# New durations, a shared port and whole groups of small products in the count that orders a decoder trunk's engines

## The chip, the core and the metric

The kernel runs on one core of a Trainium2 chip. A core has five engines that run side by side, each through its own list of instructions in a fixed order: TensorE (PE, with its weight loads as PEld), VectorE (DVE), ScalarE (ACT), GpSimd (POOL) and SyncE (SP), which issues the transfers. The metric is the device time of one execution in microseconds (us), and of several runs the median.

## What is computed

A trunk of two layers (DEPTH = 2) over 1024 tokens of width 1024. Each layer normalises, projects the tokens with one large matrix, runs three token mixers, gates and merges their outputs, and projects back. The reference, cut to what matters here:

```python
def hybrid_layer(x, c_act, positions, ...):
    mod = c_act @ w_ada + b_ada
    shift, scale, gate = jnp.split(mod[:, None, :], 3, axis=-1)
    h = rms_norm(x, norm_g) * (1.0 + scale) + shift
    proj = h @ w_in
    pool_u, pool_g, q, k, v, ret_g, rw, rw_g, gate_logits = jnp.split(proj, points, axis=-1)
    o_pool = causal_pool_mixer(pool_u, pool_w, pool_scale) * jax.nn.silu(pool_g)
    o_ret = retention(q, k, v, positions, ret_norm_g) * jax.nn.silu(ret_g)
    o_rwkv = rwkv7_time_mix(rw, shift_mu, w0, w2, a0, a2, ...) * jax.nn.silu(rw_g)
    y = jnp.einsum('btnw,nwd->btnd', jnp.stack([o_pool, o_ret, o_rwkv], axis=2), w_branch)
    merged = jnp.sum(jax.nn.sigmoid(gate_logits.reshape(B, T, N_BRANCHES, D)) * y, axis=2)
    return x + gate * (merged @ w_out)

# inside rwkv7_time_mix, after r, w, k, v, a are made
    w = -jax.nn.softplus(-(w0 + jnp.tanh(wl) @ w2)) - 0.5
    a = jax.nn.sigmoid(a0 + al @ a2)
    def step(S, inp):
        r_t, w_t, k_t, v_t, a_t, b_t = inp
        sa = jnp.einsum('bhvk,bhk->bhv', S, a_t)
        S = S * w_t[:, :, None, :] + sa[..., None] * b_t[:, :, None, :] + v_t[..., None] * k_t[:, :, None, :]
        return S, jnp.einsum('bhvk,bhk->bhv', S, r_t)
```

The output is `rms_norm(x, final_g)` after both layers.

## The kernel before

**Large products.** The projections run as fp32r products of 128 columns of weights by 512 tokens into a PSUM tile `acc` (three banks). For accuracy each is made of three: high part by high part (`wh`, `hhi`), high by low (`hlo`), low by high (`wl`). The weights come by transfer into `wr`, ScalarE casts the high part `wh`, and GpSimd subtracts to get the low part `wl`. All three have three buffers. These products are the filler: they can run whenever an `acc` bank is free and weights are ready.

**Small products.** The RetNet heads (`ret_task`) and the RWKV head pairs (`rwkv_task`) use fp32 products and transposes of 128 by 128 or less, in PSUM tiles `mx` (two banks), `two` (two banks, used in turn by `cyt()`) and `ch`. An fp32 product appears as two rows of the profile, a transpose or an fp32r product as one. A RWKV head pair goes through these stages: `prepare` (low-rank products `lora_mm`, decay sums, normalising), `scores` (the products of BK and AR into an `mx` bank named `g` for the first head and a bank of `two` for the second), `invert` (a triangular inverse on VectorE), `states` (`av`), and then a chain of 16 chunks of 64 tokens. Each chunk is a serial walk: `two` from S and AR on TensorE, `xst` on VectorE, `ch` from xst and G on TensorE, `Z` on VectorE, `ch` from Z and BKt on TensorE, the new `S` on VectorE. There are eight such head pairs, four in each of the two layers.

**Which rows of the array.** In `lora_mm` the first output's products use partitions 0 to 63 of both operands and the second output's use 64 to 127, written in turn. The products in `scores` do the same with the two heads.

**The order.** After a first part whose order is written out by hand (line 230 in the profile), the kernel doesn't emit its instructions where they are written. A class `Log` records each call as an `Op` with its engine, operands and lane ("rwkv", "mix", "post", "evac" and so on, or "" for the main flow). At the end `plan()` simulates the five engines with one estimate of occupancy and latency for each operation, from `times()`, and always takes the earliest engine and on it the ready operation with the smallest key (its place in the log, with RWKV 3000 places ahead). VectorE, ScalarE and GpSimd may hold back an operation if a RWKV one is about to be ready. `emit()` then writes the instructions in the order of the simulated starts, at line 413, which is why most rows of the profile carry that line. The chip keeps this order on each engine, whatever the real times are: an operation that comes late holds up all that stand behind it on its engine.

The estimates of TensorE before: 227 ns for an fp32r product of 512 columns, scaled down to 256 columns, 120 below; `max(n * 0.846, m * 0.8) + 3` for any fp32 product or transpose; half of that if it uses 64 rows and writes 128; and 190 ns more until a reader may start. Weight transfers count 2200 ns.

Of the kernel before, what the change touches and what calls it, by code (L numbers as in the profile page):

```python
# [10 lines left out]
F32R = mybir.dt.float32r  # L11
# [6 lines left out]
P = 128  # L18
# [78 lines left out]
ORDER = ("PE", "DVE", "ACT", "POOL", "SP")  # L97
NEXT = {"PE": 54, "DVE": 34, "ACT": 34, "POOL": 78, "SP": 60}
BIAS = {"rwkv": -3000, "evac": -500, "post": -200, "ada": 1500}


class Op:
    __slots__ = (
        "eng", "fn", "args", "kw", "outs", "ins_", "lane", "key", "n", "late", "allocs", "after", "free",
        "left", "users", "ready", "start", "end", "occ", "dur", "inst", "no_dep", "own_dep", "idx",
# [78 lines left out]
class Log:  # L184


    def __init__(self, nc, tc):
        self.nc, self.tc = nc, tc
        self.on = False
        self.ops = []  # L190
        self.tag = {}
        self.acc = {}
        self.lane = ""
        self.vector = Proxy(self, "DVE", nc.vector)
        self.scalar = Proxy(self, "ACT", nc.scalar)
        self.gpsimd = Proxy(self, "POOL", nc.gpsimd)
        self.tensor = Proxy(self, "PE", nc.tensor)
        self.sync = Proxy(self, "SP", nc.sync)

    def call(self, eng, name, real, a, k):  # L200
# [4 lines left out]
        else:  # L205
            outs, ins = aps[:1], aps[1:]
        o = Op()
        o.eng, o.fn, o.args, o.kw, o.outs, o.ins_ = eng, real, a, k, outs, ins
        o.lane, o.n, o.late, o.inst = self.lane, name, not self.on, None
        o.no_dep = o.own_dep = None  # L210
        o.after, o.free, o.allocs = {}, [], []
        o.idx = len(self.ops)
        reads = ins + (outs if name == "matmul" and k.get("start") is False else [])
        for x, w in [(x, False) for x in reads] + [(x, True) for x in outs]:
# [12 lines left out]
            self.acc[x.tensor.name] = keep  # L227
        self.ops.append(o)
        if not self.on:
            o.inst = real(*a, **k)  # L230
        return o

    def times(self, o):
        out = o.outs[0]
        n = max(x.free_size() for x in o.outs + o.ins_)
        if o.eng == "PE":
            m = o.args[1].free_size() if o.n == "transpose" else o.kw["lhsT"].free_size()
            n = out.free_size()
            rows = (o.args[1] if o.n == "transpose" else o.kw["lhsT"]).partition_size()
            if o.n != "transpose" and o.kw["rhs"].dtype == F32R:  # L240
                occ = 227 * n / 512 if n >= 256 else 120
            else:
                occ = max(n * 0.846, m * 0.8) + 3
            if rows == 64 and out.partition_size() == P:
                occ /= 2
            return occ, occ + 190
        if o.eng == "SP":
            return 340, 2200
        if o.eng == "ACT":
            d = 215 + 0.75 * n + 45 * (len(o.ins_) - 1)  # L250
            return d - 95, d
        if o.eng == "POOL":
            if o.n == "memset":
                return 60 + n, 100 + n
            if n <= 16:
                d = (1650 if n > 4 else 1010) if len(o.ins_) > 1 else 190
            else:
                d = 190 + 2.15 * n
            return d - 45, d
        if o.n == "reciprocal":  # L260
            d = 240 + 5.86 * n
            return d - 80, d
        if o.n == "transpose":
            return 1960, 2030
        if o.n == "tensor_tensor_scan":
            return 185, 265
        wide = [x for x in o.ins_ if x.free_size() == n]
        d = 155 + 1.05 * n + 45 * (len(o.ins_) - len(wide))
        if len(wide) < 2 and all(x.space != PSUM for x in o.ins_ + o.outs):
            d = 170 + 0.62 * n  # L270
        return d - 84, d

    def plan(self):
# [39 lines left out]
        for o in todo:  # L313
            for p in o.after:
                p.users.append(o)
        cand = {e: [] for e in ORDER}
        free = {e: 0.0 for e in ORDER}
# [3 lines left out]
        def offer(o):  # L321

            for t in list(o.allocs):
# [87 lines left out]
    def emit(self):  # L411
        for o in self.plan():
            o.inst = o.fn(*o.args, **o.kw)  # L413
            if o.no_dep is not None:
# [11 lines left out]
def trunk_kernel(ctx, tc, xT, cvec, pos, vecs, consts, w_ada, w_all, pool_w, lora_w, out):  # L426
# [623 lines left out]
    def ret_task(l, hd, qT, kT, vT, sg):  # L1050
# [6 lines left out]
        for h in range(2):  # L1057
            cl = lambda t, c: t[:, c * P : (c + 1) * P]
            yield wait(kT[h], qT[h])
            ps = mx("rs")  # L1060
            for c in range(4):
                mmul(cl(ps, c), lhsT=cl(kT[h], c), rhs=cl(qT[h], c), start=True, stop=True)
            sm = mo("rsm")
# [3 lines left out]
            ps = mx("rkt")  # L1067
            for c in range(4):
                trans(cl(ps, c), cl(kT[h], c))
            kt = mo("rkt")  # L1070
# [3 lines left out]
            ps = mx("rvt")  # L1074
            for c in range(4):
                trans(cl(ps, c), cl(vT[h], c))
            vt = mo("rvt")
# [3 lines left out]
            kv = mx("rkv")  # L1081
            for c in range(4):
                mmul(cl(kv, c), lhsT=cl(kt, c), rhs=cl(vt, c), start=True, stop=True)
            R = []
# [21 lines left out]
            ps = mx("rot")  # L1106
            for c in range(4):
                trans(cl(ps, c), cl(yn, c))
            ob = mo("rob")
# [5 lines left out]
    def lora_mm(pss, lw, hc, lt):  # L1115
        for i, (a, b) in enumerate(((0, 0), (0, 1), (1, 0))):
            for j in range(2):
                own = slice(64 * j, 64 * j + 64)
                mmul(pss[j], lw[a][own, hc], lt[b][own, :], start=(i == 0), stop=(i == 2))

    def rwkv_task(l, hp, kT, rT, vp, lt, lw):
# [16 lines left out]
        def prepare(h):  # L1138
# [39 lines left out]
            ps = mx("vt")  # L1178
            for c in range(4):
                trans(ps[:, c * P : (c + 1) * P], vp[h][:, c * P : (c + 1) * P])  # L1180
            for par in range(2):
# [47 lines left out]
        def scores(h):  # L1229
            yield max(until(whole[h] + 1000), wait(Z, spare=600))  # L1230
            for q in range(2):
                ps = mx("bt")
                c0 = 8 * h + 4 * q
                for c in range(4):
                    trans(ps[:, c * P : (c + 1) * P], jt(BK, slice(0, P), c0 + c), timed=True)
# [61 lines left out]
        def states():  # L1297
            for q in range(4):
                yield wait(G, Z)
                ps = mx("av")  # L1300
                for j in range(8):
                    c, hd = 4 * q + j // 2, j % 2
                    mmul(
                        ps[0:64, j * 64 : j * 64 + 64],
                        G[64:128, 16 * hd + c, 64:128],
                        Z[64:128, c, 64 * hd : 64 * hd + 64],
                    )
                nc.scalar.copy(AV[:, q * HF : (q + 1) * HF], ps[0:64, :])
# [8 lines left out]
        for q in range(2):  # L1317
            ps = mx("m1")
            for u in range(16):
                uu = 16 * q + u  # L1320
                mmul(ps[32:64, u * 32 : u * 32 + 32], G[0:32, uu, 96:128], T13[:, uu, :], timed=True)
            nc.scalar.copy(T1[32:64, q * HF : (q + 1) * HF], ps[32:64, :])
# [4 lines left out]
        for q in range(2):  # L1327
            yield max(until(left[q]), 1500.0)
            ps = mx("m2")
            for u in range(16):  # L1330
                uu = 16 * q + u
                mmul(
                    ps[0:32, u * 32 : u * 32 + 32], T1[32:64, uu * 32 : uu * 32 + 32], G[32:64, uu, 96:128], timed=True
                )
            nc.scalar.copy(
# [58 lines left out]
    def rwkv_post(l, hp, h, yn, bv):  # L1394
        yield 6500
        yield wait(yn, spare=3000)
        ps = mx("yt")
        for j in range(4):
            trans(ps[:, j * P : (j + 1) * P], yn[:, j * P : (j + 1) * P])
        ob = t_ri("wob")  # L1400
# [828 lines left out]
```

## Times and profile before

| what | value |
|---|---|
| median of 3 runs | 2561.44 us (2560.07 to 2567.08) |
| profiled execution, its own time | 2556.54 us |
| its span, first to last instruction | 2554.8 us |
| mean granted TensorE clock | 0.967 |
| busy PE / DVE / POOL / ACT | 2420.8 / 1406.0 / 890.2 / 853.1 us |
| `acc` from hhi, wh: products, mean | 1788, 408 ns |

Rows of a group name the line, engine, operation, output and inputs, shape and count, then busy time, mean of one in ns, and the idle time just before them with its releaser. Matmuls are pipelined, so the duration of a row includes the way through the array; what a product costs TensorE is the distance from its start to the next start. Rows of a timeline give start, duration, engine and operation, and in brackets the idle time before and what ended it; "xN" merges N equal neighbours.

### The profile page before, as it was taken

The page shows a single profiled execution, that of the slowest core. Times are in us where ns is not written, and L with a number is a line of the kernel's source. Part 1 is how long each engine was busy: PE and PEld are TensorE (multiplying, and loading weights), DVE is VectorE, ACT ScalarE, POOL GpSimd, SP SyncE. Part 2 cuts the span into 40 slices and gives each one's busy share as a digit, 9 for nine tenths or more (in the row PEclk, how much of TensorE's full clock was granted, in tenths as well). Part 3 has the DMA queues.
Part 4 walks back from the last instruction along what each step waited for, and adds up shares of the span by engine and source line. Part 5 has one row for each costly group of instructions (what it writes and reads, how often), then busy time and mean ns, then how long its engine had stood idle before and what let it go on. Part 6 is the DMA issues. An engine that isn't in the chain of part 4 may idle for free.

```text
span 2554.8 us, 35214 instructions
## 1 busy us (share of the span) xinstructions
PE 2420.8 (95%) x13204; PEld 1963.2 (77%) x13204; DVE 1406.0 (55%) x2666; ACT 853.1 (33%) x1567; POOL 890.2 (35%) x772
## 2 busy tenths in 40 slices
PE   5998999998999999999989998999899999999998
PEld 4776777777777778788877876788778877887888
DVE  7675663674686370335365768525664765124354
ACT  5534322322322123512344342332242223342243
POOL 4211223223223343655442222133133244365641
PEclk9997999999999999999999998999899999999999
DMA  6312002112223362564562201121012124337542
GB/s 239 113 47 70 29 26 76 30 30 76 71 64 118 104 207 84 165 221 144 165 197 85 67 26 38 31 71 47 29 64 59 59 79 148 103 114 223 174 128 75
DMA packets 138043, 248.86 MB, mean 97 GB/s; under 512 B 15632, under 2 KB 18960, under 8 KB 137872
## 3 DMA queue, kind: packets, MB, share of 16 engines
q1 hardware_dynamic: 137872, 246.61, 30.7%
q8 instruction: 104, 1.70, 0.3%
q14 instruction: 67, 0.55, 0.1%
HBM read 187.04 MB, written 59.51 MB: 97 GB/s over the span
## 4 chain that ended last, share of the span: by engine, by line
PE 63%; DVE 9%; issue 1%; ACT 1%; DMA 1%; POOL 1%; DVEq 0%; SPq 0%; ACTq 0%; POOLq 0%
PE acc L413 52%; PE two L413 2%; PE ch L413 2%; PE m L413 1%; DVE two L413 1%; PE g L413 1%; DVE tm L413 1%; PE ro L413 1%; PE av L413 1%; DVE ksq L413 1%; DVE yc L413 0%; DVE traw L413 0%; DVE hlo L413 0%; DVE ada_acc L413 0%; DVE wsum L413 0%
## 5 line engine op out<-in xcount | busy, mean ns | idle before, releaser
L413 PE MATMUL acc<-hhi,wh 128*128 128x512 f32 x1788 | 728.8, 408 | 22.0 <-ACT gsg L413 11.6
L413 POOL TENSOR_TENSOR wl<-wr,wh 128x512 fp32r<-128x512 f32 x300 | 399.7, 1332 | 949.7 <-ACT wh L413 887.9
L413 PE MATMUL acc<-hlo,wh 128*128 128x512 f32 x1788 | 722.5, 404 | 0.0
L413 PE MATMUL acc<-hhi,wl 128*128 128x512 f32 x1788 | 721.6, 404 | 0.0
L413 PEld LDWEIGHTS acc<-hhi,wh 128*128 128x128 f32 x1788 | 342.4, 192 | 92.7 <-ACT gsg L413 12.7
L413 PEld LDWEIGHTS acc<-hhi,wl 128*128 128x128 f32 x1788 | 341.5, 191 | 66.3 <-issue 2.5
L413 PEld LDWEIGHTS acc<-hlo,wh 128*128 128x128 f32 x1788 | 342.0, 191 | 65.5 <-issue 4.0
L413 ACT CAST wh<-wr 128x512 fp32r<-128x512 f32 x300 | 185.4, 619 | 616.8 <-PE acc L413 463.6
L413 DVE SCALAR_TENSOR_TENSOR S<-ch,pc,SP 64x64 f32<-64x64 f32 x256 | 72.3, 282 | 60.0 <-PE ch L413 54.0
L413 ACT COPY y<-two 64x128 f32<-64x128 f32 x128 | 33.0, 258 | 215.3 <-PE two L413 210.1
L413 DVE TENSOR_TENSOR tm<-MT,two 64x30 f32<-64x30 f32 (+14 forms) x240 | 76.7, 319 | 21.1 <-ACT two L413 13.1
L413 DVE TENSOR_TENSOR two<-two,tm 64x30 f32<-64x30 f32 (+14 forms) x240 | 79.1, 330 | 8.3
L413 DVE SCALAR_TENSOR_TENSOR gs<-gs,acc 128x512 f32<-128x512 f32 x64 | 43.8, 684 | 71.0 <-PE acc L413 68.9
L413 PE MATMUL acc<-oz,wh 128*128 128x512 f32 x256 | 80.4, 395 | 0.0
L413 PE MATMUL acc<-oy,wh 128*128 128x512 f32 x256 | 80.3, 395 | 0.0
L413 PE MATMUL acc<-oG,wh 128*128 128x512 f32 x256 | 79.1, 390 | 0.0
L413 PEld LDWEIGHTS ch<-xst,G 128*65 128x65 f32 x512 | 46.9, 146 | 37.3 <-DVE xst L413 31.8
L413 ACT ACTIVATE gsg<-acc 128x512 f32<-128x512 f32 x86 | 50.7, 593 | 71.8 <-PE acc L413 48.0
L413 POOL TENSOR_TENSOR vr<-vr,fixed 128x8 f32<-128x8 f32 (+1 forms) x32 | 44.7, 1397 | 81.3 <-DVE vr L413 77.7
L413 PE MATMUL acc<-T,wh 128*128 128x512 f32 x216 | 67.6, 394 | 5.0 <-ACT acc L413 5.0
L413 DVE TENSOR_TENSOR xst<-two,MT 64x128 f32<-64x128 f32 x128 | 37.5, 293 | 61.8 <-PE two L413 56.3
L413 PEld LDWEIGHTS two<-S,AR 128*128 128x128 f32 x256 | 44.2, 202 | 35.1 <-DVE S L413 19.2
(334 smaller groups left out, 4507.5 us busy)
## 6 DMA issues: line engine op xcount, KB each, us to landing
wr<-in_w_all SPq DMA_DIRECT2D x328, 256.0 KB, 2.7
gd<-gsg SPq DMA_DIRECT2D x96, 256.0 KB, 2.0
gs<-gd SPq DMA_DIRECT2D x96, 256.0 KB, 3.8
wada<-in_w_ada SPq DMA_DIRECT2D x70, 256.0 KB, 2.9
ol<-od SPq DMA_DIRECT2D x48, 256.0 KB, 3.0
wraw<-in_w_all SPq DMA_DIRECT2D x36, 256.0 KB, 2.8
traw<-hd SPq DMA_DIRECT2D x32, 256.0 KB, 2.9
ringG<-in_w_ada SPq DMA_DIRECT2D x26, 256.0 KB, 4.8
```

The source lines that it names most:

```text
L413: o.inst = o.fn(*o.args, **o.kw)
```

## The change

The edit is in the class `Log` and in the places where small products are written.

1. **Durations.** `pe_time` replaces the TensorE estimates: 228 ns for more than 256 columns of fp32r, 120 otherwise; an fp32 product counts twice the old formula, a transpose once; half with 64 rows and 128 output partitions, as before. A reader may start 165 ns after, not 190.
2. **Port.** An operation has a flag `port`. It is set on GpSimd operations with more than one input, on VectorE operations with two full inputs in SBUF, and on VectorE copies and scalar operations with one input from SBUF. In the simulated run an operation with the flag waits until the last one with the flag has ended.
3. **Holding back.** ScalarE and GpSimd operations of the main flow (lane "") count as ready GUARD = 500 ns later. An operation that has been ready for PATIENCE = 2500 ns is no longer held back for RWKV. A GpSimd operation outside RWKV is put off if a VectorE operation of RWKV that needs the port will be ready within 0.7 of its duration.
4. **Units.** `with nc.together():` records all calls inside it as one `Op` with the sum of their times, ready when the inputs and banks of all are ready, and emitted without a gap. It is put around the products of `lora_mm`, the transposes and products of `ret_task`, the `vt`, `bt`, score, `av`, `m1` and `m2` products of `rwkv_task`, and the transposes of `rwkv_post`.

```diff
+GUARD = 500
+PATIENCE = 2500
...
+        o = self.group if self.on else None
+        if isinstance(o, Op):
+            o.calls.append((real, a, k, name))
+            o.outs += outs
+            o.ins_ += ins
+        else:
+            o = Op()
+            o.eng, o.calls, o.outs, o.ins_ = eng, [(real, a, k, name)], list(outs), list(ins)
...
+            if self.on and self.group is not None:
+                self.group = o
...
+    def pe_time(self, n, a, k):
+        out = a[0]
+        w = a[1] if n == "transpose" else k["lhsT"]
+        f = out.free_size()
+        if n != "transpose" and k["rhs"].dtype == F32R:
+            t = 228 if f > 256 else 120
+        else:
+            t = (max(f * 0.846, w.free_size() * 0.8) + 3) * (1 if n == "transpose" else 2)
+        return t / 2 if w.partition_size() == 64 and out.partition_size() == P else t
...
-            return occ, occ + 190
+            occ = sum(self.pe_time(q, a, k) for _, a, k, q in o.calls)
+            return occ, occ + 165
...
+            o.port = len(o.ins_) > 1
...
+        sb = [x for x in o.ins_ if x.free_size() == n and x.space != PSUM]
+        o.port = len(sb) > 1 or (len(sb) == 1 and len(o.ins_) == 1 and o.n in ("tensor_copy", "tensor_scalar", "tensor_scalar_mul"))
...
+            if o.lane == "" and o.eng in ("ACT", "POOL"):
+                o.ready += GUARD
             cand[o.eng].append(o)
...
-                    t = max(free[e], min(o.ready for o in cand[e]))
+                    t = max(free[e], min(max(o.ready, port) if o.port else o.ready for o in cand[e]))
...
-            now = [o for o in c if o.ready <= t]
+            now = [o for o in c if o.ready <= t and not (o.port and port > t)]
...
-            if e != "PE" and o.occ > 100:
+            if e != "PE" and o.occ > 100 and t < o.ready + PATIENCE:
                 soon = [h for h in c if h.lane == "rwkv" and h.key < o.key and t < h.ready < t + 0.7 * o.occ]
+                if e == "POOL" and o.lane != "rwkv":
+                    other = [h for h in cand["DVE"] if h.lane == "rwkv" and h.port and h.ready < t + 0.7 * o.occ]
+                    if other:
+                        o.ready = max(t, min(h.ready for h in other)) + 300
+                        continue
...
+            if o.port:
+                port = t + o.occ
...
     def lora_mm(pss, lw, hc, lt):
-        for i, (a, b) in enumerate(((0, 0), (0, 1), (1, 0))):
-            for j in range(2):
-                own = slice(64 * j, 64 * j + 64)
-                mmul(pss[j], lw[a][own, hc], lt[b][own, :], start=(i == 0), stop=(i == 2))
+        with nc.together():
+            for i, (a, b) in enumerate(((0, 0), (0, 1), (1, 0))):
+                for j in range(2):
+                    own = slice(64 * j, 64 * j + 64)
+                    mmul(pss[j], lw[a][own, hc], lt[b][own, :], start=(i == 0), stop=(i == 2))
...
-                for j in range(4):
-                    for hd in range(2):
-                        rows = slice(64 * hd, 64 * hd + 64)
-                        mmul(gps[hd][:, j * P : (j + 1) * P], jt(BK, rows, c0 + j), jt(AR, rows, c0 + j), timed=True)
+                with nc.together():
+                    for j in range(4):
+                        for hd in range(2):
+                            rows = slice(64 * hd, 64 * hd + 64)
+                            mmul(gps[hd][:, j * P : (j + 1) * P], jt(BK, rows, c0 + j), jt(AR, rows, c0 + j), timed=True)
```

The other groups are wrapped in the same way.

More of the change, by code (lines that the diff above doesn't have):

```diff
@@ L193, in __init__ @@
         self.lane = ""
+        self.group = None
         self.vector = Proxy(self, "DVE", nc.vector)
@@ L412, in emit @@
         for o in self.plan():
-            o.inst = o.fn(*o.args, **o.kw)
+            for f, a, k, _ in o.calls:
+                o.inst = f(*a, **k)
             if o.no_dep is not None:
@@ L1060, in ret_task @@
             ps = mx("rs")
-            for c in range(4):
-                mmul(cl(ps, c), lhsT=cl(kT[h], c), rhs=cl(qT[h], c), start=True, stop=True)
+            with nc.together():
+                for c in range(4):
+                    mmul(cl(ps, c), lhsT=cl(kT[h], c), rhs=cl(qT[h], c), start=True, stop=True)
             sm = mo("rsm")
@@ L1074, in ret_task @@
             ps = mx("rvt")
-            for c in range(4):
-                trans(cl(ps, c), cl(vT[h], c))
+            with nc.together():
+                for c in range(4):
+                    trans(cl(ps, c), cl(vT[h], c))
             vt = mo("rvt")
@@ L1081, in ret_task @@
             kv = mx("rkv")
-            for c in range(4):
-                mmul(cl(kv, c), lhsT=cl(kt, c), rhs=cl(vt, c), start=True, stop=True)
+            with nc.together():
+                for c in range(4):
+                    mmul(cl(kv, c), lhsT=cl(kt, c), rhs=cl(vt, c), start=True, stop=True)
             R = []
@@ L1106, in ret_task @@
             ps = mx("rot")
-            for c in range(4):
-                trans(cl(ps, c), cl(yn, c))
+            with nc.together():
+                for c in range(4):
+                    trans(cl(ps, c), cl(yn, c))
             ob = mo("rob")
@@ L1233, in scores @@
                 c0 = 8 * h + 4 * q
[L1234 to L1235 removed]
+                with nc.together():
+                    for c in range(4):
+                        trans(ps[:, c * P : (c + 1) * P], jt(BK, slice(0, P), c0 + c), timed=True)
                 nc.scalar.copy(BKt[:, c0 : c0 + 4, :], ps.rearrange("p (c n) -> p c n", n=P))
@@ L1329, in rwkv_task @@
             ps = mx("m2")
[L1330 to L1334, printed above, removed]
+            with nc.together():
+                for u in range(16):
+                    uu = 16 * q + u
+                    mmul(
+                        ps[0:32, u * 32 : u * 32 + 32], T1[32:64, uu * 32 : uu * 32 + 32], G[32:64, uu, 96:128], timed=True
+                    )
             nc.scalar.copy(
@@ L1397, in rwkv_post @@
         ps = mx("yt")
-        for j in range(4):
-            trans(ps[:, j * P : (j + 1) * P], yn[:, j * P : (j + 1) * P])
+        with nc.together():
+            for j in range(4):
+                trans(ps[:, j * P : (j + 1) * P], yn[:, j * P : (j + 1) * P])
         ob = t_ri("wob")
```

67 lines of the change are left out of this document (35 added, 32 removed).

## The prediction

> **What bounds the kernel now.** I read the page of the profile first: the busy line, and the line of the forty slices that has TensorE's granted clock in tenths.
>
> ```profile
> span 2554.8 us, 35214 instructions
> PE 2420.8 (95%) x13204; PEld 1963.2 (77%) x13204; DVE 1406.0 (55%) x2666; ACT 853.1 (33%) x1567; POOL 890.2 (35%) x772
> ...
> PEclk9997999999999999999999998999899999999999
> ```
>
> TensorE is busy for 95% of the span and no other engine passes 55%. 134.0 us (2554.8 less 2420.8) are idle, and the clock falls below 9 tenths in three slices. So two things can shorten this kernel: less TensorE work, or less idleness and the half clock that follows it. The windows of 100 us say how much a bad stretch costs.
>
> ```profile
> 200.00:300.00 100.00, 89.93 (x418) 70.78 (x418) 60.66 (x120) 37.93 (x71) 21.38 (x24) 0.83 0.16 52
> 500.00:600.00 100.00, 97.40 (x707) 78.41 (x707) 68.75 (x177) 34.08 (x72) 25.46 (x25) 0.97 0.11 35
> ```
>
> The columns are time, then busy time of PE, PEld, DVE, ACT, POOL, then granted clock, DMA share and GB/s. From 500 us on a RWKV chain runs beside filler products: 2.6 us idle and 0.03 of 97.4 us in clock, 5.5 us lost. From 200 us on it is 10.07 idle and 0.17 of 89.93 in clock, 25.4 us lost. What the bad stretch looks like stands in its timeline (start, duration, engine, and in brackets the idle time before and its releaser):
>
> ```profile
> 222.78 0.79 PE L413 MATMUL two<-S,AR 128*128 128x128 f32 x2 [0.31 <-DVE S L413]
> ...
> 224.53 0.60 ACT L413 ACTIVATE gsg<-acc 128x512 f32<-128x512 f32 x1
> ...
> 225.18 0.80 PE L413 MATMUL acc<-hhi,wh 128*128 128x512 f32 x1 [0.41 <-ACT gsg L413]
> ```
>
> TensorE had only the serial chain to do (`two` from S and AR here). The filler product `acc` could not start until ScalarE emptied an `acc` bank into `gsg`, and `gsg` came late in ScalarE's fixed order. I call this a starved chain; against a fed one it costs 25.4 less 5.5, some 20 us. Of the eight chains (two layers, four head pairs) I count one as starved: the clock line falls below 8 in the fourth slice alone.
>
> **The change, part by part.** Nothing is computed differently. Only the order of each engine's instructions changes, so I price what neighbours in the order cost on TensorE, and then what the new count may do to waits.
>
> *The two halves of the low-rank product (`lora_mm`) as one unit.* Its six products use rows 0 to 63 and 64 to 127 in turn. The group of the first output, then two timelines of TensorE, with the halves side by side and with one half alone:
>
> ```profile
> L413 PE MATMUL lw<-lt,lw 64*128 64x512 f32 x48 | 18.4, 486 | 1.4 <-ACT lw L413 1.4
> ...
> 102.83 0.49 PE L413 MATMUL lw<-lt,lw 64*128 64x512 f32 x1
> 102.84 0.49 PE L413 MATMUL two<-lt,lw 64*128 64x512 f32 x1
> 103.17 0.39 PE L413 MATMUL lw<-lt,lw 64*128 64x512 f32 x1
> 103.17 0.39 PE L413 MATMUL two<-lt,lw 64*128 64x512 f32 x1
> 103.40 0.39 PE L413 MATMUL lw<-lt,lw 64*128 64x512 f32 x1
> 103.40 0.39 PE L413 MATMUL two<-lt,lw 64*128 64x512 f32 x1
> 103.72 0.50 PE L413 MATMUL acc<-hhi,wh 128*128 128x512 f32 x1
> ...
> 277.29 0.95 PE L413 MATMUL lw<-lt,lw 64*128 64x512 f32 x3
> 278.17 0.50 PE L413 MATMUL acc<-hlo,wh 128*128 128x512 f32 x1
> ```
>
> Side by side, six products take 103.72 less 102.83, 0.89 us. One half of three takes 278.17 less 277.29, 0.88 us, the same. Each output has 48 rows, three for each of 16 calls. In the timeline of the whole span 11 pairs share a start (the first at 86.0, the last at 1399.96 us); the other 74 of 96 rows stand alone, which are 12 of the 16 calls. As one unit they gain 12 times 0.88, **10.6 us**. Bounds: 37 pairs saved at the 0.23 us step of the rows above, 8.5, to 10.6.
>
> *The score products (`g` and `two` from AR, BK) as one unit.* This is the same shape of work, four products of rows 0 to 63 and four of rows 64 to 127, in fp32, where one product is two rows of the profile.
>
> ```profile
> L413 PE MATMUL g<-AR,BK 64*128 64x128 f32 x256 | 37.0, 285 | 0.0
> L413 PE MATMUL two<-AR,BK 64*128 64x128 f32 x256 | 36.0, 294 | 8.7 <-DVE AR L413 5.4 <-DVE BK L413 3.2
> ...
> 106.64 1.16 PE L413 MATMUL g<-AR,BK 64*128 64x128 f32 x8
> 107.72 0.50 PE L413 MATMUL acc<-hhi,wh 128*128 128x512 f32 x1
> 108.15 1.16 PE L413 MATMUL two<-AR,BK 64*128 64x128 f32 x8
> 109.24 0.50 PE L413 MATMUL acc<-hlo,wh 128*128 128x512 f32 x1
> 109.58 0.40 PE L413 MATMUL acc<-hhi,wl 128*128 128x512 f32 x1
> ```
>
> Each block of 8 takes 1.08 and 1.09 us (unmerged, its steps are 0.10 into it, 0.21, and then 0.112 a row), and no row of one half starts with a row of the other. 256 rows of 8 each are 32 blocks of each half, 2.17 us a unit. Alternated, the second row of one product can run beside the first of the next: 8 steps of 0.112, one more at the end and the head, about 1.19 us. Gain 32 times 0.98, **31.4 us**. The trace shows side by side only for the fp32r products, and their weight loads too:
>
> ```profile
> 102.83 0.18 PEld L413 LDWEIGHTS lw<-lt,lw 64*128 64x128 f32 x1 [0.36 <-issue]
> 102.83 0.18 PEld L413 LDWEIGHTS two<-lt,lw 64*128 64x128 f32 x1
> ```
>
> Bounds: 0 if fp32 rows don't overlap; below nothing if each change of half costs the longer first step (0.10 more, 8 times a unit, 32 units: a loss of 26 us). I take the gain, because loads and products of the two halves overlap in the nearest rows. The Trainium skill, page "TensorEngine Tiling (Array Packing)", section Key Properties, says that a change of the tiling mode drains the array and a change of the tile alone does not. By that the loss bound would be out and the sum would stay as it is; no run here shows it for fp32.
>
> *The other units* (four transposes, `rs`, `rkv`, `av`, `m`) sit on full rows or one corner, so nothing in them can overlap. They only stop a block from being cut, and most are whole today, so I take nothing; if the cut pieces, some 50, each cost as much as the `acc` step after a small block (109.24 to 109.58, 0.34 instead of 0.23), 5.5 us at most. A unit holds TensorE up to 1.2 us (2.2 if the halves of the scores don't overlap), and a chain product that becomes ready meanwhile waits behind it. That delays VectorE's part of the chain, and filler products keep TensorE busy until then; without fillers 32 units would cost about 1 us each.
>
> *Coupled waits.* A unit needs both its banks. Low-rank halves now wait for the later one, and the next head pair's tanh and scans with them. That delays a head pair, not TensorE, while fillers last. Some of the 42 us saved may come back as idle: the fed window above is idle 2.6% of its time and the starved one 10%, which are 1 and 4 us; I take 2.
>
> *Corrected durations.* An fp32 product counted 111 ns and 190 until a reader may start, 0.30 us; now 222 and 165, 0.39. The trace:
>
> ```profile
> 358.15 0.38 PE L413 MATMUL two<-S,AR 128*128 128x128 f32 x2
> ...
> 358.64 0.29 DVE L413 TENSOR_TENSOR xst<-two,MT 64x128 f32<-64x128 f32 x1
> ```
>
> The new number is right: the product takes 0.38. The order before was made for a TensorE faster than it is, so the others came late against it. *Port exclusion* is also real here:
>
> ```profile
> 257.55 0.69 DVE L413 SCALAR_TENSOR_TENSOR BK<-aT,ksq 128x512 f32<-128x512 f32 x1
> 257.75 1.64 POOL L413 TENSOR_TENSOR wl<-wr,wh 128x512 fp32r<-128x512 f32 x1 [4.48 <-ACT wh L413]
> 258.27 1.67 DVE L413 SCALAR_TENSOR_TENSOR BK<-BK,Lc 128x512 f32<-128x512 f32 x1
> ```
>
> The second VectorE operation is of the first one's shape but takes 1.67, because it runs against GpSimd's. *GUARD* puts weight casts later in ScalarE's order, which today blocks on them:
>
> ```profile
> ACT wh L413 <- issue: 148.0, 42, 7.5
> ```
>
> 42 waits, 148.0 us in total, for something other than an engine; a transfer is my reading. *PATIENCE* only ends such holding back. None of these four changes work; each can only move waits. The best bound is all the idle time, 134.0 us, with its clock; the worst, further starved chains at 20 us each. A better count should feed the starved chain, but it has a reason of its own (the `acc` banks), so I take half of its price, **10 us**.
>
> Sum: 10.6 + 31.4 + 10 − 2 = 50 us. The profiled execution took 2556.5 us (span 2554.8 and 1.7 around it); it becomes 2506. The median of the three runs is 2561.4, 4.9 above it: I forecast **2512**.
>
> **The rivals.** (B) *fp32 halves don't run side by side.* For it: no fp32 row in the trace does. Against: the loads above. Then 31.4 us are gone: 2543. (C) *Starved chains spread*, the slower case. With the true TensorE cost the count puts fewer fillers into a chunk of a chain. Its four hops take 2.20 us by the old formulas, 0.45 of it TensorE, so 7.7 fillers of 0.227; by the new, 2.46 with 0.90, so 6.9. The chain then reaches VectorE and the `acc` banks with less slack, and TensorE waits at each hop as at 222 us. For it: the stretch at 200 us shows how a late `gsg` feeds on itself through the half clock. Against: seven chains are fed today. It decides from the third further starved chain (60 us, more than the 50 gained); four more give 2512 + 80 = 2592. (D) *The count repairs more*: no starved chain (10 more), and a quarter of the 134 us idle gone (33): 2512 − 10 − 33 = 2469. For it: the waits of ScalarE on "issue" and the TensorE cost that was off by half are both put right. Against: what waits for a bank or a buffer stays. (E) *It doesn't do what it says*: saved TensorE time comes back as idle at the end of a stage because the fillers are spent earlier and the chain takes as long. For it: VectorE is 61 to 69% busy in the chain windows. Against: idle there is 2.6 us in 100 in the fed one. 2561.
>
> **How the numbers follow.** Forecast 0.44 (2490 to 2545 as its own range), B 0.16, C 0.21, D 0.12, E 0.07. What measurement can tell from no change is about 0.3%, 2554 to 2569. Faster: 0.44 + 0.12 + 0.14 of B, 0.70. Same: E's 0.07 and 0.02 of B, 0.09. Slower: C, 0.21. The range, 2470 to 2585, leaves out half of D (below) and half of C (above), some 0.17, and holds the unknown cost of `g` at nothing and at its loss of 26 us (2512 + 31 + 26 = 2569).
>
> **What would show it.** In the profile after: `lw` and `two` from lt always at one start, and their blocks of three gone; rows of `g` and `two` from AR, BK starting 4 ns apart, a unit in 1.2 us, not 2.2 (B if 2.2). The window around the first chain near 97% busy and clock 0.97, not 90% and 0.83 (C if more windows look like that one). ScalarE's wait of `wh` on "issue" well under 148 us for GUARD. The forecast is wrong if the busy time of PE does not fall by some 40 us, or if it does and the idle time grows by as much.

## The result, and the profile after

| | before | after |
|---|---|---|
| median (4 runs each on the same chip) | 2561.5 us | 2436.34 us (2429.15 to 2442.13) |
| ratio, 95% interval | | 0.9506 [0.9477, 0.9535] |
| span of the profiled execution | 2554.8 us | 2427.1 us |
| busy PE | 2420.8 us | 2330.2 us |
| span less busy PE | 134.0 us | 96.9 us |
| mean granted clock | 0.967 | 0.981 |

The kernel became 125 us faster. The prediction had 50 us (2512), in a range whose fast end was 2470, so the result lies outside it. One run of ten with units alone (13027.19 us) and one of four of the changed kernel with old durations (2618.02 us) were far slower than their fellows, and the medians and ratios below leave them out. First the busy line and the clock line of the changed kernel's page, which answer to the first fence of the prediction:

```profile
span 2427.1 us, 35189 instructions
PE 2330.2 (96%) x13204; PEld 1905.0 (78%) x13204; DVE 1383.2 (57%) x2666; ACT 851.6 (35%) x1567; POOL 887.5 (37%) x772
...
PEclk9999999899999999999999999999999999999999
```

TensorE does the same 13204 rows in 90.6 us less. Before, three slices were below 9 tenths; now it is one, the eighth, which was not among the three. Then three windows of 100 us of the changed kernel, in the columns of the prediction:

```profile
200.00:300.00 100.00, 95.77 (x563) 76.51 (x564) 73.67 (x153) 38.65 (x72) 29.61 (x32) 1.00 0.18 53
400.00:500.00 100.00, 85.10 (x446) 68.25 (x445) 68.13 (x127) 26.77 (x45) 22.40 (x21) 0.88 0.13 40
500.00:600.00 100.00, 97.11 (x675) 79.46 (x674) 55.45 (x129) 34.25 (x74) 30.85 (x33) 0.97 0.19 61
```

The bad stretch at 200 us (89.93 busy, clock 0.83 before) is gone. At 400 us there is a worse one than the kernel before had at that time, whose window was this:

```profile
400.00:500.00 100.00, 92.83 (x440) 73.98 (x440) 50.81 (x76) 30.47 (x54) 28.11 (x30) 0.97 0.18 56
```

One row of TensorE's timeline in the changed kernel shows the longest stop in this window:

```profile
439.83 1.09 PE L452 MATMUL bt<-cst,BK 128*128 128x128 f32 x4 [4.84 <-DVE BK L452]
```

**Where the 127.7 us of the span went.** The groups of the small products by form, in the changed kernel:

```profile
L452 PE MATMUL g<-AR,BK 64*128 64x128 f32 x256 | 38.3, 296 | 1.2 <-DVE po L452 1.0 <-ACT BKt L452 0.2
L452 PE MATMUL two<-AR,BK 64*128 64x128 f32 x256 | 37.8, 295 | 0.0
L452 PE MATMUL lw<-lt,lw 64*128 64x512 f32 x48 | 15.3, 425 | 1.1 <-ACT Z L452 0.9 <-DVE ksq L452 0.2
L452 PE MATMUL two<-lt,lw 64*128 64x512 f32 x48 | 15.3, 425 | 0.0
```

The busy times of the two halves look as large as before, but they now cover the same time: the idle time before the second half is 0.0. What they cost is seen only in the starts. The beginning and end of one score unit in TensorE's timeline, and of one low-rank unit:

```profile
1864.72 0.37 PE L452 MATMUL g<-AR,BK 64*128 64x128 f32 x1
1864.72 0.37 PE L452 MATMUL two<-AR,BK 64*128 64x128 f32 x1
1864.93 0.27 PE L452 MATMUL g<-AR,BK 64*128 64x128 f32 x1
1864.94 0.27 PE L452 MATMUL two<-AR,BK 64*128 64x128 f32 x1
...
1865.60 0.27 PE L452 MATMUL g<-AR,BK 64*128 64x128 f32 x1
1865.61 0.27 PE L452 MATMUL two<-AR,BK 64*128 64x128 f32 x1
1865.81 0.50 PE L452 MATMUL acc<-hhi,wh 128*128 128x512 f32 x1
...
87.75 0.49 PE L452 MATMUL lw<-lt,lw 64*128 64x512 f32 x1
87.76 0.49 PE L452 MATMUL two<-lt,lw 64*128 64x512 f32 x1
...
88.31 0.39 PE L452 MATMUL lw<-lt,lw 64*128 64x512 f32 x1
88.32 0.39 PE L452 MATMUL two<-lt,lw 64*128 64x512 f32 x1
88.63 0.50 PE L452 MATMUL acc<-hhi,wbig 128*128 128x512 f32 x1
```

Sixteen fp32 rows of two halves take 1865.81 less 1864.72, 1.09 us, where each half alone took 1.08. Summed from each start to the next over all rows of the trace, the 512 score rows cost 71.6 us before and 37.5 after, and the 96 low-rank rows 29.0 and 16.1. That is 34.1 + 12.9 = 47.0 us. (Such a distance includes idle time behind a row; with each row counted to its own end at most, it is 46.0.) Idle TensorE time fell by 37.1 us. The other 43.6 of the 90.6 us of busy time lie in products that are the same in number and in cost at full clock (a large product's start to the next start has a median of 227 ns in both). An estimate of the clock's part is 2554.8 times 0.033 less 2427.1 times 0.019, 38 us. So some 47 us are TensorE work, and some 75 are idleness and the half clock that follows it (in the kernel before, each window of 10 us from 200 to 230 us has a granted clock of 0.50, with TensorE busy for 5.97, 7.55 and 8.24 us). Some 5 us of the span are left over.

### The profile page after: what moved, and what is told of

It reads as the page before. It is cut to its first block, busy times and chain, and to the rows that moved or that the text cites. A ratio compares the mean times of both kernels' runs of the same rounds, so it can differ in the third digit from the quotient of the medians.

```text
span 2427.1 us, 35189 instructions
## 1 busy us (share of the span) xinstructions
PE 2330.2 (96%) x13204; PEld 1905.0 (78%) x13204; DVE 1383.2 (57%) x2666; ACT 851.6 (35%) x1567; POOL 887.5 (37%) x772
## 4 chain that ended last, share of the span: by engine, by line
PE 83%; DVE 11%; ACT 2%; DMA 2%; issue 2%; POOL 1%; SPq 0%; DVEq 0%; ACTq 0%; POOLq 0%
PE acc L452 69%; PE ch L452 3%; PE two L452 3%; DVE ksq L452 1%; PE m L452 1%; PE g L452 1%; PE av L452 1%; PE ro L452 1%; DVE BK L452 1%; DVE Lc L452 1%; DVE S L452 1%; PE rkv L452 1%; PE bt L452 1%; PE rs L452 1%; DMA wada<-in_w_ada 1%
## 5 line engine op out<-in xcount | busy, mean ns | idle before, releaser
L452 PE MATMUL acc<-hhi,wh 128*128 128x512 f32 x1788 | 722.9, 405 | 17.5 <-DVE rot L452 12.7
L452 PE MATMUL acc<-hhi,wl 128*128 128x512 f32 x1788 | 718.6, 402 | 0.0
L452 POOL TENSOR_TENSOR wl<-wr,wh 128x512 fp32r<-128x512 f32 x300 | 401.2, 1339 | 852.7 <-ACT wh L452 801.0
L452 PE MATMUL acc<-hlo,wh 128*128 128x512 f32 x1788 | 712.8, 399 | 0.0
L452 PEld LDWEIGHTS acc<-hhi,wh 128*128 128x128 f32 x1788 | 340.6, 190 | 81.0 <-DVE rot L452 10.8
L452 PEld LDWEIGHTS acc<-hhi,wl 128*128 128x128 f32 x1788 | 339.5, 190 | 64.3 <-issue 0.7
L452 PEld LDWEIGHTS acc<-hlo,wh 128*128 128x128 f32 x1788 | 339.8, 190 | 62.9 <-issue 1.8
L452 ACT CAST wh<-wr 128x512 fp32r<-128x512 f32 x300 | 185.3, 618 | 490.5 <-PE acc L452 329.2
L452 DVE SCALAR_TENSOR_TENSOR S<-ch,pc,SP 64x64 f32<-64x64 f32 x256 | 72.5, 283 | 59.0 <-PE ch L452 55.3
L452 ACT COPY y<-two 64x128 f32<-64x128 f32 x128 | 33.0, 258 | 190.4 <-PE two L452 185.6
L452 ACT ACTIVATE gsg<-acc 128x512 f32<-128x512 f32 x86 | 50.8, 595 | 116.3 <-PE acc L452 100.9
L452 DVE SCALAR_TENSOR_TENSOR gs<-gs,acc 128x512 f32<-128x512 f32 x64 | 43.8, 684 | 81.3 <-PE acc L452 75.4
L452 DVE TENSOR_TENSOR tm<-MT,two 64x30 f32<-64x30 f32 (+14 forms) x240 | 76.5, 319 | 14.2 <-ACT two L452 6.8
L452 DVE TENSOR_TENSOR two<-two,tm 64x30 f32<-64x30 f32 (+14 forms) x240 | 79.0, 329 | 7.5
L452 PE MATMUL acc<-oz,wh 128*128 128x512 f32 x256 | 80.5, 395 | 0.0
L452 PE MATMUL acc<-oy,wh 128*128 128x512 f32 x256 | 80.2, 395 | 0.0
L452 DVE SCALAR_TENSOR_TENSOR xres<-acc,mod,xres 128x512 f32<-128x512 f32 (+1 forms) x40 | 25.7, 643 | 94.1 <-PE acc L452 94.1
L452 PE MATMUL acc<-oG,wh 128*128 128x512 f32 x256 | 79.2, 390 | 0.0
L452 DVE COPY Z<-ch 64x128 f32<-64x128 f32 x128 | 36.0, 281 | 61.3 <-PE ch L452 60.7
L452 PEld LDWEIGHTS ch<-xst,G 128*65 128x65 f32 x512 | 44.3, 141 | 33.8 <-DVE xst L452 30.9
L452 POOL TENSOR_TENSOR rkl<-ka,rkh 128x512 fp32r<-128x512 f32 x16 | 20.7, 1292 | 136.2 <-ACT rkh L452 127.4
L452 DVE TENSOR_TENSOR xst<-two,MT 64x128 f32<-64x128 f32 x128 | 37.5, 293 | 56.0 <-PE two L452 51.9
```

Source lines behind the costliest of these rows:

```text
L452: o.inst = f(*a, **k)
```

## The experiments

L413 and L452 are the same line: the loop that emits the order. Where a run is told as "before and one part", it is the changed kernel with the other parts switched off; with all of them off, the order of each engine is that of before. The switches: no units is `log.group = None`; old durations are the estimates of before; no port is `o.port = False`, which also ends the deferral on GpSimd, since no operation has the flag; no holding limit is `PATIENCE = 1e12`. Medians are in us, and the ratios are to before.

### The units by themselves, and the count by itself

```diff
-GUARD = 500
-PATIENCE = 2500
+GUARD = 0
+PATIENCE = 1e12
...
-            return occ, occ + 165
+            return occ, occ + 190
...
-            o.port = len(o.ins_) > 1
+            o.port = False
...
-                if e == "POOL" and o.lane != "rwkv":
+                if False:
```

> The units alone, with the old durations and no port, guard or holding rule. All theories: low-rank products 16 us and scores 37 us of TensorE as in the changed kernel, 47 us less than before. Theory 1 (the true fp32 cost removed the waits): idle time and half clock stay as before, 2514 us. Theory 2 (the units removed the waits, too, because blocks are no longer cut and halves no longer hold banks apart): near the changed kernel, 2445. Theory 3 (port, guard and holding rules removed them): 2514.

```diff
-                log.group = True
+                log.group = None
```

> All of the new count, but no units. Low-rank products 29 us and scores 71 us of TensorE as before. Theory 1 (durations) and theory 3 (port, guard, holding): the waits are gone and only the 47 us of TensorE time are missing, 2483 us. Theory 2 (units): waits as before, 2550 to 2561.

Units alone (with the old durations): 2558.72, 0.9989 [0.9977, 1.0002], which none of the theories had. The count alone: 2482.05, 0.9693 [0.9673, 0.9713]. The units save TensorE work here too: from each start to the next, score rows take 44.6 us and low-rank rows 16.5, some 40 us less than before. None of it reaches the end. Two windows of the kernel with units alone:

```profile
400.00:500.00 100.00, 85.14 (x427) 67.52 (x426) 47.61 (x77) 30.31 (x54) 26.12 (x27) 0.86 0.15 48
500.00:600.00 100.00, 74.80 (x557) 62.30 (x557) 59.89 (x159) 26.00 (x58) 16.02 (x17) 0.78 0.09 27
```

The stretch from 500 us, fed before with 97.40, has 74.80 and a clock of 0.78. TensorE's idle time grew from 134.0 to 173.8 us, and the busy time fell by only 34.7. The waits took it all. So the larger part of the gain comes from the count, and what it does is to keep TensorE fed: with the count alone the window at 200 us is busy for 97.50 us and the one at 500 us for 98.84.

### Which part of the count

```diff
-PATIENCE = 2500
+PATIENCE = 1e12
...
-                log.group = True
+                log.group = None
...
-            o.port = len(o.ins_) > 1
+            o.port = False
```

> The kernel before with the new TensorE durations alone. Theory 1 (durations): some 75 us of waits gone, 2486 us. Theory 2 (units) and theory 3 (port, guard, holding): 2561, within 10. If any new order moves the time by tens of us (theory 4), it may be anywhere from 2500 to 2600.

```diff
-            t = 228 if f > 256 else 120
+            t = 227 * f / 512 if f >= 256 else 120
...
-            return occ, occ + 165
+            return occ, occ + 190
```

> The changed kernel with the old TensorE durations (a unit has the sum of its parts). Theory 1 (durations): the 75 us of waits come back, 2511 us. Theory 2 (units) and theory 3 (port, guard, holding): 2436, within 10.

The new durations by themselves (GUARD also at 0): 2573.0, 1.0042 [1.0022, 1.0063]. The changed kernel with the old ones: 2437.32, 0.9518 [0.9497, 0.9539], the same as with the new. The corrected durations, which the change is named after first, give nothing; by themselves they cost 11 us.

```diff
-PATIENCE = 2500
+PATIENCE = 1e12
```

> The changed kernel without PATIENCE alone (an operation may be held back for RWKV without limit). Theory P (PATIENCE fed the chains: without it ScalarE and GpSimd operations ready for long, gsg above all, are held while a chain's operations keep coming): starved chains come back, TensorE idle over 130 us and clock near 0.95, 2500 to 2560 us. Theory G (GUARD) and theory X (port and the deferral of GpSimd): 2436, within 10.

```diff
-GUARD = 500
+GUARD = 0
...
-                log.group = True
+                log.group = None
...
-            return occ, occ + 165
+            return occ, occ + 190
...
-            o.port = len(o.ins_) > 1
+            o.port = False
```

> The kernel before with PATIENCE alone: old durations, no units, no port, no guard. Theory P: the waits go, 2480 to 2500 us, with low-rank and score products costing TensorE what they did before. Theory G and theory X: 2561, within 10.

```diff
-GUARD = 500
+GUARD = 0
```

> The changed kernel with GUARD = 0. Theory G: waits come back, 2490 to 2520 us. Theory P and theory X: 2436, within 10; ScalarE's waits of wh on what the profile calls issue (150 us in the changed kernel) stay where they are.

```diff
-            o.port = len(o.ins_) > 1
+            o.port = False
```

> The changed kernel with no operation needing the port, and so no deferral of GpSimd. Theory X: waits come back, 2490 to 2520 us. Theory P and theory G: 2436, within 10.

Without PATIENCE the changed kernel takes 2479.38, 0.9676 [0.9658, 0.9695]: 43 us of the gain are gone. PATIENCE alone on the kernel before gives 2477.84, 0.9671 [0.965, 0.9692], 83 us, as much as the whole count without the units (2482.05). Without GUARD: 2434.79, 0.9505 [0.9484, 0.9526], no change. Without the port: 2450.79, 0.9562 [0.9542, 0.9581], 14 us slower. That GUARD does nothing can be read in ScalarE's waits of the changed kernel as well:

```profile
ACT wh L452 <- issue: 150.1, 42, 6.1
```

The 42 waits that it was to relieve took 148.0 us before, and 157.6 (44 waits) in the changed kernel without GUARD.

### The parts that carry the gain, put together

```diff
-GUARD = 500
+GUARD = 0
...
-            return occ, occ + 165
+            return occ, occ + 190
...
-            o.port = len(o.ins_) > 1
+            o.port = False
```

> The kernel before with the units and PATIENCE, and nothing else of the count (old durations, no port, no guard, no deferral of GpSimd). Theory P (PATIENCE feeds the chains, 83 us alone, and the units save 47 us of TensorE time): 2561 less 130, 2431 us, the changed kernel's time or a little below. Theory X (port and deferral are worth 14 us beside PATIENCE): 2450.

```diff
-GUARD = 500
-PATIENCE = 2500
+GUARD = 0
+PATIENCE = 1e12
...
-            return occ, occ + 165
+            return occ, occ + 190
```

> Units, port and deferral of GpSimd, without PATIENCE, GUARD and the new durations. The changed kernel without PATIENCE took 2479 us, units alone 2560. If port and deferral are the second cure of the starved chains: 2480 to 2490 us. If GUARD or the durations are (theory G, theory 1): 2540 to 2560.

Units and PATIENCE: 2455.73, 0.9586 [0.9572, 0.9601]. Port and its deferral on top of these are the 18 to 21 us that lead to 2437.32 (with GUARD, old durations) or 2434.79 (new durations, no GUARD). Units and port without PATIENCE: 2507.08, 0.979 [0.9774, 0.9806], 52 us less than units alone and between the two expectations. So port with its deferral is a second, weaker cure: idle TensorE time is 146.0 us here and 173.8 with units alone. From there to the changed kernel without PATIENCE, 2479.38, are 28 us more, by GUARD and durations in that company. Which of the two gives them was not told apart.

### What the holding limit frees

The rule in `plan()` holds a long operation back if a RWKV one will be ready within 0.7 of its duration. My theory was that on VectorE the short steps of a chain or of `invert` come without end, so that a long operation is held again and again.

```diff
-            if e != "PE" and o.occ > 100 and t < o.ready + PATIENCE:
+            if e != "PE" and o.occ > 100 and (e != "DVE" or t < o.ready + PATIENCE):
```

> The kernel before with PATIENCE on VectorE alone. Theory PV (it is VectorE's held operations that matter: the pool mixer's difference pd and the rope steps, which keep the mo buffers that gsg needs): 2478 us, as with PATIENCE on all engines. Theory PA (ScalarE's holding of gsg itself): 2561, within 10.

PATIENCE on VectorE alone, with everything else as before: 2478.03, 0.9669 [0.9647, 0.9691], the whole effect. What is held, and what follows, stands in the timeline of the kernel before, ahead of the `gsg` at 224.53 us that the prediction shows:

```profile
134.91 0.68 DVE L413 SCALAR_TENSOR_TENSOR ang<-nrot,ang 128x512 f32<-128x512 f32 x1
150.65 1.07 POOL L413 TENSOR_TENSOR pt<-pu 128x527 f32<-128x527 f32 x1
174.64 0.69 DVE L413 SCALAR_TENSOR_TENSOR ang<-nrot,ang 128x512 f32<-128x512 f32 x1
193.46 0.47 PE L413 MATMUL acc<-hhi,wl 128*128 128x512 f32 x1
214.75 0.26 ACT L413 COPY y<-two 64x128 f32<-64x128 f32 x1 [3.22 <-PE two L413]
218.63 0.26 ACT L413 COPY y<-two 64x128 f32<-64x128 f32 x1 [3.15 <-PE two L413]
221.10 0.67 DVE L413 SCALAR_TENSOR_TENSOR pd<-pt,pu 128x512 f32<-128x512 f32 x1
```

GpSimd makes the pool mixer's `pt` at 150.65. VectorE reads it, for `pd`, 70 us later; two steps `ang` of one rotary angle, 0.7 us each, stand 40 us apart. `pt` and `pd` lie in buffers of the ring `mo`, of which there are four, and the gate `gsg` needs one too. The last large product into `acc` before the stop starts at 193.46, so the input of the `gsg` of 224.53 was ready some 30 us before it. ScalarE was free: it stood idle for 3 us at a time in front of `y`. The order simply had `gsg` behind those. The count itself, `plan()` of the kernel before, says why, in its own simulated time, which is not the chip's: `pd` is ready at 59.8 us; first it stands behind `silu` and the `ang` steps, which the rule holds up too, then, between further `ang` steps, the rule holds `pd` itself back 13 times, and it is placed at 105.7. The `gsg` asks for a buffer at 77.9. Two of the four are free, but `offer()` gives a ring's buffers out in the order of the log, and `pdh` and `pdl`, the high and low part that are made from `pd`, stand ahead of it there. So the two free ones are kept for them, and `gsg` is let through only when `pd` has released `pt`, at 107.1. In the kernel with PATIENCE alone the same operations:

```profile
150.67 1.06 POOL L452 TENSOR_TENSOR pt<-pu 128x527 f32<-128x527 f32 x1
177.44 0.59 ACT L452 ACTIVATE gsg<-acc 128x512 f32<-128x512 f32 x1
178.67 0.68 DVE L452 SCALAR_TENSOR_TENSOR pd<-pt,pu 128x512 f32<-128x512 f32 x1
...
200.00:300.00 100.00, 97.17 (x511) 76.34 (x511) 60.34 (x122) 40.16 (x75) 28.77 (x30) 1.00 0.19 54
```

`pt` at the same time, `pd` 42 us earlier, and the window 97.17 busy at full clock. (`gsg` can stand ahead of `pd` here, because the buffer that it is given is one that had been free all along.) Some 28 us still lie between `pt` and `pd`: in that kernel's count the `ang` steps ahead of `pd` are still held, each for no longer than the limit. In the changed kernel the wait is 16 us:

```profile
139.34 1.06 POOL L452 TENSOR_TENSOR pt<-pu 128x527 f32<-128x527 f32 x1
...
155.08 0.67 DVE L452 SCALAR_TENSOR_TENSOR pd<-pt,pu 128x512 f32<-128x512 f32 x1
```

The rows show when things happen, not that the buffer is the link. So I broke the link in the kernel before without touching the holding, in two ways: `gsg` from another ring, and a fifth `mo` buffer.

```diff
-            s = mo("gsg")
+            s = t_ri("gsg")
```

> The kernel before with the gate's output gsg in a buffer of the ring ri (14) and not of mo (4), and nothing else changed. Theory M (held VectorE operations starve TensorE through the mo buffers): the stretch of 185 to 230 us with no filler product goes, granted clock from 200 to 300 us above 0.95, 2500 to 2540 us. If the mo buffers are not the link: 2561, within 10, with the same starved stretch.

```diff
-    t_ri = slot("ri", 14)
+    t_ri = slot("ri", 13)
...
-    t_mo = slot("mo", 4, HF + 16)
+    t_mo = slot("mo", 5, HF + 16)
```

> The kernel before with five mo buffers and, to make room, 13 ri buffers instead of 14. Theory M (mo buffers are the link): part of the starved chains is fed, 2520 to 2550 us. If they are not: 2561 or slower for the missing ri buffer.

`gsg` from the ring `ri`: 2522.47, 0.9844 [0.9826, 0.9861], and the window is fed under the holding rule of before:

```profile
200.00:300.00 100.00, 98.74 (x493) 76.97 (x492) 52.32 (x99) 34.90 (x65) 31.92 (x32) 1.00 0.19 60
```

Five `mo` buffers: 2549.62, 0.9951 [0.9936, 0.9966]. So the ring `mo` is a link, and taking the gate out of it is worth 39 us; a fifth buffer brings 11. The edit moves the pool mixer as well: without gates ahead of it in the ring, `pt` runs at 105.0 us and `pd` at 124.6. So the 39 us belong to the whole new order, and not to the one wait of `gsg` for `pd`. It is not all of PATIENCE's 83 us; through which operations the rest goes is open. One candidate does not pass through `mo`: `silu`, which VectorE makes from an `acc` bank that it thereby frees, comes at 166.66 us in the kernel before, 28 us after its ScalarE half (139.00), and with PATIENCE alone 3 us after it (142.04 and 138.57).

```diff
-            s = mo("gsg")
+            s = t_ri("gsg")
```

> The changed kernel with gsg in the ring ri instead of mo. Theory M with PATIENCE already in: the mo buffers bind little more, 2425 to 2440 us. If buffers still bind TensorE's idle 62 us inside the stages: 2400 to 2420.

The same in the changed kernel: 2461.05, 0.9602 [0.9576, 0.9628]. It is 25 us slower, which neither expectation had. A likely reason, which no run shows, is that the ring `ri` serves RWKV, and where little is held the gate only takes its buffers.

### How much is chance of the order

Any change of a number in the count deals a new order, so a gain could be luck. Five nanoseconds more until a reader may start, in both kernels:

```diff
-            return occ, occ + 190
+            return occ, occ + 195
```

> The kernel before with 195 ns instead of 190 until a reader may start, a change of no meaning that gives another order. Theory 4 (any new order moves the time): anywhere from 2530 to 2600 us. The other theories: 2561, within 10.

```diff
-            return occ, occ + 165
+            return occ, occ + 170
```

> The changed kernel with 170 ns instead of 165. Theory 4 (any new order moves the time): 2436 by tens of us either way. The other theories: 2436, within 10.

2560.09, 0.9996 [0.9985, 1.0006], and 2442.64, 0.9532 [0.9512, 0.9551]. That is 1 and 6 us, small beside 43 or 83, though not beside the 14 us of the port. Five nanoseconds are a small push: the new durations, a larger one, moved the kernel before by 11 us.

### Less holding still

```diff
-PATIENCE = 2500
+PATIENCE = 1000
```

> The changed kernel with PATIENCE 1000 instead of 2500. Theory P: what is held for less than 2.5 us matters little to the buffers, 2425 to 2445 us; if holding is a loss at any length, 2400 to 2425.

```diff
-PATIENCE = 2500
+PATIENCE = 0
```

> The changed kernel with PATIENCE 0: nothing is held back for RWKV, and GpSimd isn't put off. Theory P with holding of no use: 2420 to 2440 us. If a short hold is worth something to the chains: 2445 to 2470, as without port and deferral or slower.

2415.06, 0.9428 [0.9398, 0.9457], and 2416.82, 0.9427 [0.9398, 0.9456]; the second holds nothing and defers nothing. Both are faster than the changed kernel by some 20 us, with intervals that don't meet its own. The stretch at 400 us, with a limit of 1000 ns and with none:

```profile
400.00:500.00 100.00, 84.44 (x443) 68.09 (x442) 63.97 (x126) 26.30 (x44) 23.76 (x22) 0.91 0.14 41
...
400.00:500.00 100.00, 100.00 (x567) 82.42 (x566) 54.52 (x88) 31.72 (x53) 27.73 (x28) 1.00 0.16 48
```

Without holding the window is full; the 1000 ns version gains elsewhere and keeps the bad stretch. That does not show that holding makes it. The same window is fed as well in the changed kernel without the port (95.89 busy, clock 0.98), without units (97.58, 1.00), without any limit on holding (94.15, 0.98) and with `gsg` in the ring `ri` (100.00, 1.00). In the runs of the changed kernel it is bad when units, port and a limit come together with `gsg` in `mo`; why is open. Holding VectorE, ScalarE and GpSimd back for RWKV earns nothing measurable here at any length that was run.

## Why the prediction was right and wrong

**The direction and the TensorE work were right.** The low-rank unit had 10.6 us and saved 12.9; the score unit had 31.4 and saved 34.1. The halves of the scores overlap even more than in the chosen working, which let the second row of one product run beside the first of the next, 1.19 us a unit: the rows start in pairs, and a unit takes 1.09. The fear of a longer first step at each change of half did not come true. The 5 us that both fell short lie mostly in the kernel before: I priced whole blocks there (32 times 2.17 is 69.4 us, and 4 times 0.89 and 12 times 1.77 is 24.8), and rows of blocks that were cut, with some idleness behind them, made it 71.6 and 29.0. Rival B, halves one after the other, is out. The other units were priced at nothing and were not tried by themselves.

**The mis-sized term is the waits: 10 us, less 2 given back, where about 75 were gained.** Three steps of the prediction led there.

1. "`gsg` came late in ScalarE's fixed order", and the count "has a reason of its own (the `acc` banks)". The row was read right and followed one step too short. The banks were full because `gsg` had not run; `gsg` had not run because in the count two `mo` buffers were taken (`pt`, `pd`) and the other two kept for what follows `pd`; and that stayed so because the count held `pd` back on VectorE, 70 us behind `pt` where the limit leaves 28. The row that says so is `pd` at 221.10, 3 us ahead of the `gsg` I quoted, and ScalarE's idle 3 us in front of `y` say that ScalarE was not the one that was late.
2. "*PATIENCE* only ends such holding back." It was counted with three changes that can only move waits, at half of one starved chain, some 10 us for all. By itself it is worth 83, and on VectorE alone as much (2478.03).
3. One starved chain of eight, by the clock line. The holding cost more than the slices below 8 tenths show: the 134.0 us of idle time were the bound of which the prediction spoke, and with PATIENCE alone 88.3 were left, in a kernel without one unit.

**Durations.** "The new number is right" was right, and that a right number brings a better order was wrong: +0.4% alone, and nothing in the changed kernel. Whether they are part of the 28 us in the kernels without PATIENCE is open. **GUARD** was to bring ScalarE's `wh` wait well under 148 us; it is 150.1. **Port** was real, and with the deferral it is worth 14 to 21 us. **Coupled waits** were taken at 2 us. In company they can't be seen, but in the kernel with units alone idleness grows by 39.8 us. That is rival E, "saved TensorE time comes back as idle", for the units alone: it said 2561, and they take 2558.72. Whether the units' coupled banks or the longer block of TensorE do that was not tried.

**The rivals.** D, "the count repairs more" (2469), came nearest, yet its cause, ScalarE's waits on issue and the true TensorE cost, is not what happened. C, starved chains that spread, does occur, in the kernel with units alone, from 400 to 600 us, but with the old durations, so by another way than C's; the saved 40 us are lost there, and with PATIENCE beside the units 22 are kept.

**The additive sum was itself a mistake.** The units are worth 3 us on the order before, with an interval that includes none, 22 beside PATIENCE (2477.84 to 2455.73) and 46 beside the whole count (2482.05 to 2436.34). In these runs, TensorE work that is saved became time only where TensorE was fed.

## What to carry to other kernels

When the bottleneck waits for a buffer, follow it back to the operation that keeps the buffer, or for which the buffer is kept, and ask whether that one waited for data or was held by the order. An engine that idles while its next operation's input was long ready is the mark of the second. A rule that lets a favoured lane hold others back needs a limit, since a serial chain always has something coming; try it with no holding at all first, which was as fast here as any limit. Before summing the gains of an edit, ask of each whether the stage where it falls is fed: work saved in a starved stage is given back as waiting.

## What the hardware showed beyond the question

Two fp32 products on the two halves of the array rows run wholly side by side: 16 rows in 1.09 us against 8 rows of one half in 1.08, with starts that differ by 0 to 0.01 us, in spite of the two rows that each fp32 product makes. The kernel before had shown it for the fp32r products only. Not every unit is so short: in the one at 104.14 us of the changed kernel the second half started 0.42 us after the first, and the unit took 1.51 us.
